# Attention and state-space background work of a hybrid decoder step: wider table products, softmax scaling and masks partly on ScalarE, sample values laid out by dimension, larger portions

## The chip, the cores and the metric

One core of one Trainium2 chip. The metric is the device time of one execution in microseconds, from the first to the last instruction with what lies around it, as the median of several runs.

## The reference

One layer of a decoder for 512 prompt tokens behind 16 meta tokens (528 rows) and 8 sample tokens (each one new position with its own cache), with shared weights, all in float32:

```python
xn = rmsnorm(x, norm_gain)                       # 536 rows of 2048
h = xn @ w_in                                    # 2048 x 8704
q, k, v, z_a, u, z_s, g_a, g_s = split(h)        # 16 query heads and 4 key heads of 64
q, k = rope(rmsnorm(q)), rope(rmsnorm(k))
# attention: window of 128, 16 meta tokens always visible, one sink per head
s = where(mask, q @ k.T / 8, -inf)
m = maximum(max(s), sink)
w = exp(s - m) / (sum(exp(s - m)) + exp(sink - m))
o = w @ v                                        # prompt in blocks of 128; a sample token: 16 + 127 + 1 keys
# S5 branch: 64 groups of 16 channels, 64 complex states each
h_t = lam_bar * h_(t-1) + b_bar @ u_t
y = gelu(real(c @ h_t) + d_skip * u)
y = y * sigmoid(y @ w_glu + b_glu)
br_a = (o * silu(z_a)) @ w_attn_out
br_s = (y * silu(z_s)) @ w_ssm_out
out = x + (sigmoid(g_a) * br_a + sigmoid(g_s) * br_s) @ w_out
```

Returned are `out` of prompt and sample, the last keys and values of the prompt, the shifted caches of the sample, and the final states.

## The kernel before

**The main line** is a long row of matrix products on TensorE. Activations lie with features on the partitions and the tokens as columns, in two halves of 268 (260 where the meta tokens are left out). Each float32 operand is split in a rounded high part and a rest (`xh`, `xl`; `whi` by ScalarE in L784, `wlo` by VectorE in L785), and a product is three matmuls: high by high, low by high, high by low. A weight tile of 128 x 1024 comes from `Stream` (L784, L785) with three buffers and two tiles ahead. Between them lies a **half unit**: one weight tile, 8 x 3 x 2 = 48 matmuls (L901). `ORDER1` lists which output blocks are made in which order: `x` blocks (gates, two half units each; evacuated to DRAM by `evac`), `u` blocks (input of the state space) and `h` blocks (keys, values, queries; `heads`, which holds a square `t` until its pair is there). What `ORDER1` leaves of the 48 x blocks follows; then come the GLU (8 half units), the state-space output (16), the attention output (16), and the last product L1264, in an arrangement with seven products for eight.

**Background.** Everything else hangs on that line by `Background`. Its lanes are generators: a step after each half unit grants a budget (`BUDGET` 4.0 while `ORDER1` runs, then `BUDGET2` 3.6, `BUDGET3` 2.2, `BUDGET4` 3.4), and portions are taken from lane 0, then lane 1, until the granted credit is used; each `yield` tells what the portion before it cost, and `yield None` ends a lane's turn. Lane 0 has the state-space preparation, eight `ssm` (one for each u block: `ssm_consts`, `ssm_block` and the gelu), `attention`, and at the end `attended`, which multiplies and splits the attention output. Lane 1 has `sample`. Instructions are put in each engine's queue by a scheduler that follows its own time line (`schedule_with_timeline_sim=True`); where two are ready, that of the earlier program text goes first. The weights' loads, casts and rests and the evacuations are given priority. Blocks `with self.later()` go behind the last matmul of the half unit just issued.

**State space.** For each u block, `ssm_consts` builds among other things the rotation table `tab` by outer products (`outer`, L297, on `rt1`, `rt2`), and `ssm_block` projects (L345, L346), rotates, scans, rotates back and projects out (L388 to L396).

**Attention.** `attention` starts when the pool of the state space is given back: it loads constants, the key rows (`keys`: `load`, `rope`, split into `KH`, `KL`), the values (`values`: copies `vb`, `mt`, five transposes on TensorE in L505 and L506, then `V`, `Vm`) and the queries of a head group (`load_q`, `queries`: `QT`). The row buffers `sb`, `sw`, `rb` are double. For each of 4 head groups and 4 blocks, `blocks` runs: `scores` (L537, L538: matmuls, copied to `S`, the previous block's part merged by mask), `softmax` (maximum, `Exp` with sums on ScalarE in L556, division into `Pn`, `Pm`), `turn` (transposes in L573, L574; `po` the own block's masked part, `pm` the meta part by head, `pp` the previous block's part) and `weigh` (L591: 4 matmuls for each of `po`, `pm`, `pp`). `weigh` of a block comes one portion after its `turn`, `turn` after the next block's `scores`.

**Sample.** `sample` has 128 rows (8 tokens by 16 heads). Keys come in 16 loads of 9 positions on the POOL queue (`load`, L677), are multiplied and summed (L685, L686); softmax; values come in 16 loads of 9 positions, are multiplied (L701), summed over a strided view (L703) and added up (L705).

Of the kernel before, what the change touches and what calls it, by code (L numbers as in the profile page):

```python
# [14 lines left out]
P = 128  # L15
# [208 lines left out]
def ssm_consts(nc, pool, psum, R, D, ub, a_bT, a_bN, a_cT, bdm):  # L224
# [70 lines left out]
    def outer(dst, i, j):  # L295
        for a in range(4):
            v.tensor_tensor(out=dst[:, a], in0=bc(x[:, i, a], 2, 12), in1=bc(y[:, j, a], 1, 11), op=ALU.mult)  # L297
# [4 lines left out]
    yield 2.3  # L302
# [11 lines left out]
    yield 2.3  # L314
# [106 lines left out]
class Attn:  # L421
    def __init__(self, nc, pool, psum, dram, C, oT, raw, rk, rq, later):
# [3 lines left out]
        self.V = [pool.tile([P, 256], F32, name=f"V{i}", bufs=1) for i in range(4)]  # L426
# [7 lines left out]
        self.QT = {}  # L434
# [91 lines left out]
    def scores(self, kv, b):  # L526
# [6 lines left out]
        for j in range(2):  # L533
# [8 lines left out]
            prev = ps[:, :, 0:128] if b else bc(C["neg"], 1, 2)  # L542
# [3 lines left out]
    def softmax(self, kv, S):  # L546
# [17 lines left out]
        v.tensor_tensor(out=Pn, in0=S[:, :, 16:144], in1=bc(den, 2, P), op=ALU.mult)  # L564
# [3 lines left out]
    def turn(self, kv, b, Pn, Pm):  # L568
# [9 lines left out]
        v.tensor_tensor(out=self.pm[0:64], in0=bc(ps[0:64, 1, 0:128], 1, 4), in1=bc(C["bd64"], 2, P), op=ALU.mult)  # L578
        parts = [(self.V[b], po), (self.Vm, self.pm)]
        if b:  # L580
            pp = pool.tile([P, 4, P], F32, name="pp", bufs=1)
            v.tensor_tensor(out=pp, in0=pt, in1=po, op=ALU.subtract)
            parts.append((self.V[b - 1], pp))
        return parts

    def weigh(self, kv, b, parts):
        nc = self.nc
        pv = self.psum.tile([P, 2, 512], F32, name="aux")
        for i, (V, pr) in enumerate(parts):
            for e in range(2):  # L590
                nc.tensor.matmul(pv[64 * e:64 * e + 64, 0, 0:256], lhsT=V[:, 64 * kv:64 * kv + 64], rhs=pr[:, e::2],  # L591
                                 start=(i == 0), stop=(i == len(parts) - 1))
# [4 lines left out]
    def blocks(self, kv, last):  # L597

        for b in range(4):
# [7 lines left out]
            if held:  # L607
                with self.later():
                    parts = self.turn(*held, *self.P)
                yield 1.8  # L610
                yield None
                with self.later():
                    self.weigh(*held, parts)
            self.P = self.softmax(kv, S)
            yield 2.0
        if last:
# [3 lines left out]
            yield 1.8  # L620
# [4 lines left out]
    def sample(self, a_sink, a_kc, a_vc):  # L625
# [48 lines left out]
        def load(i, c, src):  # L674
            t = pool.tile([P, CK, 64], F32, name="cache")
            n = CK if c < 15 else CK - 1
            self.after = nc.gpsimd.dma_start(out=t[:, 0:n], in_=src[:, c * CK:c * CK + n]).ins  # L677
            if n < CK:
                new = self.kD[i].rearrange("s b (e d) -> (s b e) d", e=2)
                for r in range(4):  # L680
                    nc.gpsimd.dma_start(out=t[r::4, n], in_=new)
            return t
        for c in range(16):
            t = load(0, c, a_kc)
            v.tensor_tensor(out=t, in0=t, in1=bc(self.qv, 1, CK), op=ALU.mult)  # L685
            v.tensor_reduce(out=s[:, c * CK:(c + 1) * CK], in_=t, axis=AX.X, op=ALU.add)  # L686
            yield 1.3
# [10 lines left out]
        op = pool.tile([P, 64], F32, name="o_p", bufs=1)  # L698
# [740 lines left out]
```

## Time and profile before

| | |
|---|---|
| three runs | 1316.38, 1316.45, 1317.16 us, median 1316.45 |
| profiled execution | 1317.95 us, its span 1316.1 us |
| PE, weight loads | busy 1300.7 and 1259.9 us |
| DVE | 1003.5 us in 1882 instructions |
| ACT, POOL | 443.5 and 52.4 us |
| granted clock of TensorE | 0.997 on average |
| DMA | 209.70 MB, 159 GB/s on average |

PE is TensorE, DVE VectorE, ACT ScalarE, POOL GpSimd, SP the engine whose queue issues most transfers. A row of a group of instructions reads: line, engine, operation, written tile <- read tiles, shape, count | busy time in all, mean of one in ns | idle time of the engine just before them and who ended it. A busy time counts overlapping instructions once, so a pipelined matmul has a mean of some 285 ns and starts every 120. The chain of waits follows the program back from its end; a piece of it is given as start, length, engine, line, count.

### The profile page before, as it was taken

Reading aid. Unit: us, or ns where it says so; the run is one execution under the profiler, and the core shown is the slowest. Engines: PE = TensorE matmul, PEld = TensorE weight load, DVE = VectorE, ACT = ScalarE, POOL = GpSimd, SP = SyncE. Lnnn points to the kernel's source line nnn. Section 1 sums busy time; section 2 is a strip of 40 time slices with the busy share of each in tenths; the row PEclk is TensorE's granted clock in tenths of the full one; section 3 lists DMA queues with packets and bytes.
Section 4 is the critical chain, followed back from the end, with each engine's and each line's share of the span. In section 5 each row is a group of like instructions: output and inputs, shape, how many; then the busy total and the mean of one; then the engine's idle time right before and its main releaser. Section 6 shows DMA issues by size and latency. Waiting matters only on the chain.

```text
span 1316.1 us, 26574 instructions
## 1 busy us (share of the span) xinstructions
PE 1300.7 (99%) x10804; PEld 1259.9 (96%) x10804; DVE 1003.5 (76%) x1882; ACT 443.5 (34%) x742; POOL 52.4 (4%) x124
## 2 busy tenths in 40 slices
PE   9999999999999999999989999999999999999998
PEld 8999999999999999999989999999999999999998
DVE  7887788887969697968577688686885357888775
ACT  8322221223222222222254433334433133344342
POOL 0000000000000000000400210100011000000000
PEclk9999999999999999999989999999999999999999
DMA  8347363626353444343874346446677666554441
GB/s 268 123 136 212 104 186 115 187 92 184 110 166 116 155 122 153 97 152 125 190 228 131 107 153 193 131 133 205 194 226 247 203 194 189 159 199 142 151 145 50
DMA packets 95962, 209.70 MB, mean 159 GB/s; under 512 B 16556, under 2 KB 34972, under 8 KB 95808
## 3 DMA queue, kind: packets, MB, share of 16 engines
q1 hardware_dynamic: 91168, 194.11, 46.8%
q0 software_dynamic: 4672, 13.89, 4.0%
q8 instruction: 85, 1.39, 0.4%
q14 instruction: 37, 0.30, 0.1%
HBM read 175.32 MB, written 34.74 MB: 160 GB/s over the span
## 4 chain that ended last, share of the span: by engine, by line
PE 91%; DMA 3%; DVE 2%; ACT 1%; SPq 1%; issue 0%; POOL 0%; DVEq 0%; POOLq 0%; ACTq 0%
PE mm L901 70%; PE pr L1264 12%; PE aux L591 2%; PE mm L988 1%; DMA sw<-rawD 1%; PE aux L537 1%; PE aux L345 1%; PE aux L346 1%; PE aux L538 1%; PE aux L1065 1%; PE mm L1186 1%; PE aux L392 1%; PE aux L573 1%; DMA gD<-z 1%; DMA sb<-rawD 0%; ACT xh L979 0%
## 5 line engine op out<-in xcount | busy, mean ns | idle before, releaser
L901 PE MATMUL mm<-xh,whi 128*128 128x260 f32 (+1 forms) x2048 | 421.4, 286 | 0.0
L901 PE MATMUL mm<-xh,wlo 128*128 128x260 f32 (+1 forms) x2048 | 417.6, 285 | 0.0
L901 PE MATMUL mm<-xl,whi 128*128 128x260 f32 (+1 forms) x2048 | 416.3, 284 | 0.0
L784 ACT CAST whi<-raw 128x1024 fp32r<-128x1024 f32 (+3 forms) x188 | 186.1, 995 | 520.8 <-PE mm L901 346.7
L901 PEld LDWEIGHTS mm<-xh,whi 128*128 128x128 f32 x2048 | 318.2, 189 | 9.7 <-issue 9.3
L901 PEld LDWEIGHTS mm<-xl,whi 128*128 128x128 f32 x2048 | 318.5, 189 | 3.9 <-issue 3.9
L901 PEld LDWEIGHTS mm<-xh,wlo 128*128 128x128 f32 x2048 | 316.1, 188 | 4.2 <-issue 4.1
L785 DVE TENSOR_TENSOR wlo<-raw,whi 128x1024 fp32r<-128x1024 f32 (+3 forms) x188 | 215.5, 1151 | 43.8 <-ACT whi L784 41.8
L1264 PE MATMUL pr<-cb,whi 128*128 128x260 f32 x896 | 161.8, 283 | 1.3 <-DVE t L1244 1.3
L1264 PEld LDWEIGHTS pr<-cb,whi 128*128 128x128 f32 x896 | 138.1, 188 | 2.1 <-ACT whi L840 1.7
L901 PE MATMUL mm<-Y,whi 128*128 128x260 f32 x768 | 125.5, 284 | 0.0
L1264 PE MATMUL pr<-cb,wlo 128*128 128x260 f32 x448 | 125.5, 283 | 0.0
L901 PEld LDWEIGHTS mm<-Y,whi 128*128 128x128 f32 x768 | 105.7, 188 | 2.3 <-issue 2.3
L841 DVE TENSOR_TENSOR wlo<-raw,whi 128x1024 fp32r<-128x1024 f32 x56 | 67.1, 1223 | 23.0 <-ACT whi L840 21.3
L1264 PEld LDWEIGHTS pr<-cb,wlo 128*128 128x128 f32 x448 | 84.0, 188 | 0.0
L901 PE MATMUL mm<-A,whi 128*128 128x260 f32 x512 | 82.2, 282 | 0.0
L901 PE MATMUL mm<-Y,wlo 128*128 128x260 f32 x384 | 77.6, 283 | 0.0
L840 ACT CAST whi<-raw 128x1024 fp32r<-128x1024 f32 x56 | 57.7, 1049 | 55.1 <-DVE raw L839 21.0
L901 PEld LDWEIGHTS mm<-A,whi 128*128 128x128 f32 x512 | 70.2, 188 | 0.0
L928 DVE TENSOR_TENSOR z<-mm,R 128x520 f32<-128x520 f32 x43 | 30.0, 697 | 44.1 <-PE mm L901 42.5
L901 PEld LDWEIGHTS mm<-Y,wlo 128*128 128x128 f32 x384 | 59.2, 188 | 0.4 <-issue 0.4
L901 PE MATMUL mm<-A,wlo 128*128 128x260 f32 x256 | 51.6, 283 | 0.0
(377 smaller groups left out, 1496.6 us busy)
## 6 DMA issues: line engine op xcount, KB each, us to landing
raw<-in_w SPq DMA_DIRECT2D x202, 512.0 KB, 3.8
gD<-z SPq DMA_DIRECT2D x48, 260.0 KB, 2.2
t<-gD SPq DMA_DIRECT2D x32, 260.0 KB, 2.8
cache<-in_kc POOLq DMA_DIRECT2D x15, 288.0 KB, 3.5
cache<-in_vc POOLq DMA_DIRECT2D x15, 288.0 KB, 3.3
xr<-in_x SPq DMA_DIRECT2D x16, 268.0 KB, 5.5
sD<-z SPq DMA_DIRECT2D x16, 260.0 KB, 2.1
z<-sD SPq DMA_DIRECT2D x16, 260.0 KB, 3.0
```

Of the source, the lines that this page charges most:

```text
L345: nc.tensor.matmul(bu[:, i, 0:272], lhsT=D["bh"][:, i, a], rhs=U[:, a], start=True, stop=False)
L346: nc.tensor.matmul(bu[:, i, 0:272], lhsT=D["bl"][:, i, a], rhs=U[:, a], start=False, stop=True)
L392: nc.tensor.matmul(y[32 * a:32 * a + 32, 0, 0:NE], lhsT=D["cl"][:, a, i], rhs=H[:, a, i, 0:NE], start=False, stop=(i == 1), skip_group_che ...
L537: nc.tensor.matmul(ps[:, e, 0:272], lhsT=q, rhs=KH[:, k0:k0 + 272], start=True, stop=False)
L591: nc.tensor.matmul(pv[64 * e:64 * e + 64, 0, 0:256], lhsT=V[:, 64 * kv:64 * kv + 64], rhs=pr[:, e::2], start=(i == 0), stop=(i == len(part ...
L784: nc.scalar.copy(out=hi, in_=raw)
L785: self.dve = nc.vector.tensor_tensor(out=lo, in0=raw, in1=hi.bitcast(F32), op=ALU.subtract).ins
L840: nc.scalar.copy(out=hi, in_=t)
L841: nc.vector.tensor_tensor(out=lo, in0=t, in1=hi.bitcast(F32), op=ALU.subtract)
L901: m = nc.tensor.matmul(ps[:, c, 0:W], lhsT=wt[:, k], rhs=xo(kt, c), start=f, stop=l)
L928: v.tensor_tensor(out=z, in0=ps, in1=R_[:, :, 8:CH], op=ALU.mult)
L1264: nc.tensor.matmul(bank, lhsT=wt[:, p], rhs=cb[p][:, e, x], start=first and f and p == 0, stop=l and p == 7, skip_group_check=not first an ...
```

## The change

Five parts.

- `outer` in `ssm_consts` makes one product of 528 elements instead of four of 132.
- `Pn` is made by four scaled copies on ScalarE instead of one product on VectorE; so is `pm`. `pp` is now a plain copy of the whole transposed block on ScalarE, no longer its difference from `po`; in exchange `po` is weighed with the differences of the V rows, `V[b] - V[b-1]`, made once per head group (`dV`, one buffer, on VectorE). `neg` has one column.
- Sample values lie by dimension: a load brings 4 dimensions of 143 positions, product and sum run over contiguous elements, and the new position's value (`vn`) is added at the end.
- Declared costs: table portions 2.3 to 2.1, `turn` 1.8 to 0.8, sample 1.3 to 1.5. Budgets: 4.0 to 4.6 and 3.6 to 4.0.
- `ORDER1`: a u block after every four blocks instead of every five. Eight more x blocks come after the list.

```diff
     def outer(dst, i, j):
-        for a in range(4):
-            v.tensor_tensor(out=dst[:, a], in0=bc(x[:, i, a], 2, 12), in1=bc(y[:, j, a], 1, 11), op=ALU.mult)
+        v.tensor_tensor(out=dst, in0=bc(x[:, i], 3, 12), in1=bc(y[:, j], 2, 11), op=ALU.mult)
...
-    yield 2.3
+    yield 2.1
...
-        self.V = [pool.tile([P, 256], F32, name=f"V{i}", bufs=1) for i in range(4)]
+        self.VV = pool.tile([P, 4, 256], F32, name="V", bufs=1)
+        self.V = [self.VV[:, i] for i in range(4)]
...
-            prev = ps[:, :, 0:128] if b else bc(C["neg"], 1, 2)
+            prev = ps[:, :, 0:128] if b else C["neg"].unsqueeze(2).to_broadcast([P, 2, P])
...
-        v.tensor_tensor(out=Pn, in0=S[:, :, 16:144], in1=bc(den, 2, P), op=ALU.mult)
+        for r in range(4):
+            nc.scalar.activation(out=Pn[:, r], in_=S[:, r, 16:144], func=AF.Copy, scale=den[:, r:r + 1])
...
-        v.tensor_tensor(out=self.pm[0:64], in0=bc(ps[0:64, 1, 0:128], 1, 4), in1=bc(C["bd64"], 2, P), op=ALU.mult)
-        parts = [(self.V[b], po), (self.Vm, self.pm)]
+        for r in range(4):
+            nc.scalar.activation(out=self.pm[0:64, r], in_=ps[0:64, 1, 0:128], func=AF.Copy, scale=C["bd64"][:, r:r + 1])
+        parts = [(self.D[kv][b], po), (self.Vm[:, 64 * kv:64 * kv + 64], self.pm)]
         if b:
             pp = pool.tile([P, 4, P], F32, name="pp", bufs=1)
-            v.tensor_tensor(out=pp, in0=pt, in1=po, op=ALU.subtract)
-            parts.append((self.V[b - 1], pp))
+            nc.scalar.copy(out=pp, in_=pt)
+            parts.append((self.V[b - 1][:, 64 * kv:64 * kv + 64], pp))
...
-                yield 1.8
+                yield 0.8
                 yield None
                 with self.later():
                     self.weigh(*held, parts)
+            if b == 0:
+                ks = slice(64 * kv, 64 * kv + 64)
+                dv = self.pool.tile([P, 3, 64], F32, name="dV", bufs=1)
+                self.nc.vector.tensor_tensor(out=dv, in0=self.VV[:, 1:4, ks], in1=self.VV[:, 0:3, ks], op=ALU.subtract)
+                self.D[kv] = [self.VV[:, 0, ks]] + [dv[:, i] for i in range(3)]
...
+        new = [kD[i].rearrange("s b (e d) -> (s b e) d", e=2) for i in range(2)]
+        vn = pool.tile([P, 64], F32, name="vn", bufs=1)
+        for r in range(4):
+            nc.gpsimd.dma_start(out=vn[r::4], in_=new[1])
...
         for c in range(16):
-            t = load(1, c, a_vc)
-            v.tensor_tensor(out=t, in0=t, in1=bc(s[:, c * CK:(c + 1) * CK], 2, 64), op=ALU.mult)
-            dst = op if c else o[:, 0]
-            v.tensor_reduce(out=dst, in_=t.rearrange("p k d -> p d k"), axis=AX.X, op=ALU.add)
-            if c:
-                v.tensor_tensor(out=o[:, 0], in0=o[:, 0], in1=op, op=ALU.add)
-            yield 1.3
+            t = pool.tile([P, 4, NK - 1], F32, name="cache")
+            self.after = nc.gpsimd.dma_start(out=t, in_=a_vc[:, 4 * c:4 * c + 4]).ins
+            v.tensor_tensor(out=t, in0=t, in1=bc(s[:, 0:NK - 1], 1, 4), op=ALU.mult)
+            v.tensor_reduce(out=o[:, 0, 4 * c:4 * c + 4], in_=t, axis=AX.X, op=ALU.add)
+            yield 1.5
+        v.scalar_tensor_tensor(out=o[:, 0], in0=vn, scalar=s[:, NK - 1:NK], in1=o[:, 0], op0=ALU.mult, op1=ALU.add)
...
-BUDGET = 4.0
-BUDGET2, BUDGET3, BUDGET4 = 3.6, 2.2, 3.4
+BUDGET = 4.6
+BUDGET2, BUDGET3, BUDGET4 = 4.0, 2.2, 3.4
...
-for _u in range(8):
-    ORDER1 += [("u", _u), ("x", 0), ("x", 0)]
-    ORDER1 += [("h", 2 * _u), ("h", 2 * _u + 1)] if _u < 6 else [("x", 0), ("x", 0)]
+for _u in range(0, 8, 2):
+    ORDER1 += [("u", _u), ("x", 0)] + [("h", 3 * _u // 2 + i) for i in range(2)]
+    ORDER1 += [("u", _u + 1), ("x", 0), ("x", 0), ("h", 3 * _u // 2 + 2)]
```

The host's layout of the value cache and the order of the weight tiles follow.

More of the change, by code (lines that the diff above doesn't have):

```diff
@@ L673, in sample @@
         s = pool.tile([P, NK], F32, name="ssc", bufs=1)
[L674 removed]
+        new = [kD[i].rearrange("s b (e d) -> (s b e) d", e=2) for i in range(2)]
+        vn = pool.tile([P, 64], F32, name="vn", bufs=1)
+        for r in range(4):
+            nc.gpsimd.dma_start(out=vn[r::4], in_=new[1])
+        for c in range(16):
             t = pool.tile([P, CK, 64], F32, name="cache")
             n = CK if c < 15 else CK - 1
[L677 removed]
+            nc.gpsimd.dma_start(out=t[:, 0:n], in_=a_kc[:, c * CK:c * CK + n])
             if n < CK:
[L679 removed]
                 for r in range(4):
[L681 to L684, printed above, removed]
+                    nc.gpsimd.dma_start(out=t[r::4, n], in_=new[0])
             v.tensor_tensor(out=t, in0=t, in1=bc(self.qv, 1, CK), op=ALU.mult)
             v.tensor_reduce(out=s[:, c * CK:(c + 1) * CK], in_=t, axis=AX.X, op=ALU.add)
[L687 removed]
+            yield 1.5
         m = pool.tile([P, 4], F32, name="m")
```

16 lines of the change are left out of this document (8 added, 8 removed).

## The prediction

> **What bounds the kernel now.** I read the page first, then TensorE's waits, then the busy times by stretches, then the chain of waits in the attention stage.
>
> ```profile
> span 1316.1 us, 26574 instructions
> PE 1300.7 (99%) x10804; PEld 1259.9 (96%) x10804; DVE 1003.5 (76%) x1882; ACT 443.5 (34%) x742; POOL 52.4 (4%) x124
> PE aux L505 <- DVE vb L501: 5.3, 1, 5.3
> PE aux L537 <- DVE QT L522: 1.3, 1, 1.3
> PE pr L1264 <- DVE t L1244: 1.3, 1, 1.3
> 991.85 149.95 PE mm L901 x1248
> 400.00:420.00 20.00, 20.00 (x159) 18.67 (x159) 19.86 (x31) 6.12 (x9) 0.35 (x3) 1.00 0.34 107
> 115.00:625.00 510.00, 510.00 (x4377) 492.29 (x4376) 416.20 (x825) 135.32 (x169) 3.26 (x28) 1.00 0.46 140
> 655.40:661.10 5.70, 0.43 (x5) 0.22 (x3) 5.37 (x12) 2.60 (x7) 0.00 (x0) 0.77 0.84 265
> 661.00:665.30 4.30, 4.26 (x20) 4.22 (x21) 4.16 (x10) 3.02 (x9) 0.00 (x0) 0.50 0.66 196
> 690.00:890.00 200.00, 200.00 (x1607) 185.81 (x1606) 151.10 (x286) 76.08 (x202) 21.01 (x40) 1.00 0.45 140
> 890.00:992.00 102.00, 102.00 (x830) 96.19 (x829) 79.35 (x136) 42.52 (x94) 8.07 (x15) 1.00 0.69 215
> 1140.00:1160.00 20.00, 18.66 (x149) 17.92 (x149) 18.96 (x23) 9.96 (x12) 0.00 (x0) 1.00 0.47 168
> ```
>
> (The stretches' columns: length, then busy time of PE, weight loads, DVE, ACT, POOL, then granted clock, DMA share, GB/s.) TensorE is the bound in every stage. Undisturbed it starts a matmul every 149.95 / 1248 = 0.120 us, and it is idle for only 1316.1 - 1300.7 = 15.4 us of the span. VectorE at 76% is not the bound: at 400 to 420 us it is busy 19.86 of 20 us and TensorE still loses nothing. So an instruction taken from VectorE gains nothing by itself. The change can move the time in two ways: by idle time of TensorE, and by how its matmuls are interleaved.
>
> The one large loss in the middle is the start of attention. TensorE stands 5.3 us before the transposes of `values` (L505). When it resumes, it runs 4.3 us at a granted clock of 0.50 and gets 20 matmuls done where 4.3 / 0.120 = 36 would fit: another 16 x 0.120 = 1.9 us. With the 1.3 us before L537 the place costs 5.3 + 1.9 + 1.3 = 8.5 us. The clock falls after 5.3 us of idleness; the 1.3 us before L1264 lie in the stretch from 1140 us, which keeps 1.00. The Trainium skill (TensorE: Matmul & The Clock Gate, Part 1: The HAM clock gate) says that one idle window of about 3.4 us halves the clock until a busy window has passed; the trace agrees, between 1.3 us without a fall and 5.3 us with one.
>
> **Work that only moves between engines or in time.** The rows of one instruction:
>
> ```profile
> L785 DVE TENSOR_TENSOR wlo<-raw,whi 128x1024 fp32r<-128x1024 f32 x80 | 97.4, 1218 | 17.1 <-ACT whi L784 17.1
> L297 DVE TENSOR_TENSOR rt<-T,T 128x132 f32<-128x132 f32 x128 | 29.2, 288 | 0.1
> L350 DVE TENSOR_TENSOR p<-aux,tab 128x528 f32<-128x528 f32 x32 | 22.5, 704 | 23.0 <-PE aux L346 22.2
> L564 DVE TENSOR_TENSOR Pn<-S,den 128x512 f32<-128x512 f32 x16 | 11.0, 690 | 0.4
> L577 DVE TENSOR_TENSOR po<-aux,k_mown 128x512 f32<-128x512 f32 x16 | 11.0, 686 | 9.2 <-PE aux L574 9.2
> L578 DVE TENSOR_TENSOR pm<-aux,k_bd 64x512 f32<-64x512 f32 x16 | 10.8, 672 | 0.0
> L582 DVE TENSOR_TENSOR pp<-aux,po 128x512 f32<-128x512 f32 x12 | 8.1, 676 | 0.0
> L703 DVE TENSOR_REDUCE o_p<-cache 128x64 f32<-128x576 f32 x15 | 17.8, 1186 | 0.1
> L686 DVE TENSOR_REDUCE ssc<-cache 128x9 f32<-128x576 f32 x16 | 11.9, 746 | 0.1
> L705 DVE TENSOR_TENSOR o_s<-o_s,o_p 128x64 f32<-128x64 f32 x15 | 3.3, 218 | 0.1
> L594 ACT COPY oT<-aux 128x128 f32<-128x128 f32 x32 | 6.9, 267 | 30.7 <-PE aux L591 30.7
> L930 ACT ACTIVATE z<-z 128x520 f32<-128x520 f32 x16 | 10.2, 637 | 3.3 <-DVE z L928 3.2
> ```
>
> Rotation tables: 128 products of 132 elements (29.2 us) become 32 of 528, at L350's 22.5 us: VectorE saves 6.7 us. Sample values: the reduction over a strided view (1186 ns) becomes one over contiguous elements, taken as L686's 746 ns: 16 x 0.44 = 7.0 us, and L705's 3.3 us go; one fused add comes. Attention: `Pn`, `pm` and `pp` leave VectorE, 11.0 + 10.8 + 8.1 = 29.9 us; four small differences of V rows (`dV`) come, under 0.7 us each by L564. ScalarE gets 64 + 64 scaled copies of 128 columns at L594's 0.267 us and 12 copies of 512 at L930's 0.637: 34.2 + 7.6 = 41.8 us. All these are worth nothing on TensorE's path as long as that has matmuls ready: its number of instructions is unchanged. `dV` has one buffer, so its write waits for the `weigh` of the head group before; behind it on VectorE stand the maximum of the next softmax and the next `wlo`, three times, and `wlo` is made two weight tiles (2 x 48 x 0.120 = 11.5 us) ahead. The POOL queue keeps its 40 loads for the sample; the four of `vn` wait for `kD` and stand ahead of later key loads, which serve only that off-path lane.
>
> Larger portions: a state-space block declares 38.6 before and gets 10 half units of 4.0; afterwards two declare 76.4 and get 16 of 4.6, with the rest running over. Counting the portions through, the first of attention comes after half unit 78 instead of 90, that of the first scores after 85 instead of 97, and attention's last after 122 instead of 141. In the state-space stage VectorE has 416.2 us of work in 510 us (82%). Afterwards 12 half units (12 x 48 x 0.120 = 69 us) are gone from the stage, and of the work 6.7 us of products, 12 x 1.22 = 14.6 of `wlo` and, for six x blocks with two operations of L564's 0.69 each, 8.3: 387 of 441 us, 88%. That is below the 99% at which the stretch from 400 us loses nothing. Heads of a pair now stand up to three blocks apart and hold one of the two `t` buffers; evacuating through the other takes 0.64 + 2 x 0.69 us of a block's 11.5, so nothing. In attention, ScalarE has 76.1 + 42.5 = 118.6 us of work in 302 us (39%); afterwards at most 160 us in 37 / 44 of that time, 254 us: 63%. Its `whi` casts have the 11.5 us of cover. I take 0 for all of this, with 3 us against as the other end: two waits such as those before L537 and L1264.
>
> **What does reach TensorE: `weigh` in fewer stretches.** In the chain of waits each uninterrupted run of `weigh` matmuls (L591) is one piece:
>
> ```profile
> 699.23 0.58 PE aux L591 x4
> ...
> 849.78 0.58 PE aux L591 x4
> 850.36 0.43 PE mm L901 x2
> 850.79 0.58 PE aux L591 x4
> 851.38 0.55 PE mm L901 x3
> 851.93 0.58 PE aux L591 x4
> ...
> 970.25 1.45 PE aux L591 x12
> ...
> 986.28 0.58 PE aux L591 x4
> ```
>
> A block's 12 records take 1.45 us in one go, and 3 x 0.58 = 1.74 in three. Between them two main matmuls take 0.43 instead of 0.24, and three 0.55 instead of 0.36. So being split in three costs 0.29 + 0.19 + 0.19 = 0.67 us, 0.33 per interruption. From the first row to the last I count 36 pieces for 16 blocks, so at most 20 interruptions can go: 6.6 us. They come from VectorE making `po`, `pm`, `pp` one after the other: ready 0.69, 1.36 and 2.03 us after the transposes, while one group occupies TensorE 0.58 us. Afterwards `po` stays on VectorE (0.69) and `pm` runs beside it on ScalarE (4 x 0.267 = 1.07): ready before `po`'s group ends at 1.27, so the first interruption can close. `pp` follows `pm` on ScalarE (1.07 + 0.64 = 1.71) and would be ready before the second group ends at 1.85. Against this, a `whi` cast or an exponential can stand in ScalarE's queue between them, and scheduled order, not readiness alone, decides. Between 0 and 20 I take 9, about half: 9 x 0.33 = 3.0 us. The other end is a loss of the same kind: ten more pieces if ScalarE makes `pm` late, 3.3 us.
>
> The Trainium skill (ScalarE: Activation LUTs, Rules for kernel authors) speaks against the move: multiplications and additions belong on VectorE, and ScalarE is for functions. For the single operation the rows agree: 4 x 0.267 = 1.07 us on ScalarE against 0.69 for `Pn`. By the rule the sum would have a loss in place of the 3.0 us, as rival 4 prices it.
>
> **The start of attention.** The stall is a queue of transfers:
>
> ```profile
> sw<-rawD SPq DMA_DIRECT2D x8, 67.0 KB, 6.9
> 657.10 3.37 DMA sb<-rawD
> 660.49 0.49 DVE L501 COPY vb<-sb 128x256 f32<-128x256 f32 x2 [0.27 <-DMA sb<-rawD]
> 667.25 0.49 DVE L501 COPY vb<-sb 128x256 f32<-128x256 f32 x2
> ```
>
> The key rows take 6.9 us to land among the constants, the first sample caches and the weights; `values` needs the buffers that the keys free. All of that starts when the state-space pool is released, in both kernels, with the same loads and the same two buffers. `keys`, `values` and `load_q` keep their portions and their text. So I leave the 8.5 us where they are, only some 70 us earlier. Their place in TensorE's order comes from the scheduler that fixes the queues when the program is built, by its own durations, so the stall can come out otherwise: the bounds are all of it gone and rival 3's growth.
>
> **The sum.** The profiled execution took 1317.95 us, 1.85 around its span, and 1.5 (0.11%) above the median of 1316.45. 1317.95 - 3.0 = 1314.95 for a profiled execution, and 1313.5 us against the median, 0.23% faster. Differences below 0.2% (2.6 us) I count as no change: about what a measurement of this kernel can tell.
>
> **Rivals.**
> 1. *Forecast* (0.42): stall kept, 5 to 14 interruptions closed: 1311.8 to 1314.8 us.
> 2. *The stall goes* (0.16). The transposes land later in TensorE's order, or the rows earlier. Short of the idle time that halves the clock, about 5.3 + 1.9 = 7 us go; the wait before L537 is next. With the 3 us of merging 1306 us, without it 1309. For it: the stall rests on a mismatch of a few us between order and transfers. Against: nothing in the chain of transfers is changed.
> 3. *The stall grows* (0.24), the case on the slower side. Both `values` portions now fall after the same half unit (81), before after 93 and 94. If TensorE's order puts the second five transposes right behind the first, it waits from the end of the first copies (660.98) to that of the second (667.74), less five transposes at half clock (5 x 4.3 / 20 = 1.1 us): 5.7 us, then 1.9 more at half clock, and the wait before L537 again: 1313.5 + 5.7 + 1.9 + 1.3 = 1322.4 us. It decides once the second wait is longer than the 3 us that merging gives. Against: the first transposes already stood where their data was expected, not where they were issued.
> 4. *ScalarE becomes late* (0.06): 41.8 / 16 = 2.6 us more ScalarE work per block; if a tenth shows on TensorE, 4.2 us in all, without merging: 1320.7 us. Against: at most 63% load and 11.5 us of cover. This is how the rule of the Trainium skill (ScalarE: Activation LUTs, Rules for kernel authors) would come out.
> 5. *Nothing reaches TensorE* (0.12): the pieces stay near 36 and the stall as it is: 1316.5 us, within 2 us.
>
> **How the numbers follow.** Of the forecast's 0.42 I put 0.12 above 1313.8 us, within 0.2%. Faster: 0.30 + 0.16 = 0.46. Same: 0.12 + 0.12 = 0.24. Slower: 0.24 + 0.06 = 0.30. The range runs from rival 2 with merging to rival 3, 1306 to 1322 us. The forecast's own range is 1311 to 1316.
>
> **What would show it.** In the changed profile: TensorE still at 99% with its 10804 instructions; the L591 pieces of the chain counted, 27 by the forecast, above 34 wrong; the wait before the transposes of `values` again 4 to 7 us, with one stretch at clock 0.50; VectorE's busy time down by 35 to 50 us and ScalarE's up by about 42; no wait of TensorE on `whi`, `pm` or `pp` above 1 us; the last `weigh` before the last of the 48 x blocks. A new wait of more than 3 us anywhere after the warm-up, or a second stretch at half clock, makes the prediction wrong on the slow side.

## The result, and the profile after

The changed kernel takes **1326.32 us** (median of 4 runs, 1325.37 to 1327.07) beside 1316.41 us for the kernel before on the same chip: a ratio of 1.0075, 95% interval 1.0057 to 1.0092. It is 9.9 us slower. The forecast was 1313.5 us with a range of 1306 to 1322, so the time lies outside the range, on the slower side.

The profiled execution took 1326.37 us. Its span and busy times, from the page of the changed kernel:

```profile
span 1324.6 us, 26577 instructions
PE 1304.9 (99%) x10804; PEld 1259.5 (95%) x10804; DVE 967.9 (73%) x1732; ACT 484.1 (37%) x882; POOL 52.3 (4%) x124
```

The engines' work moved as forecast: VectorE has 35.6 us less (forecast 35 to 50 less), ScalarE 40.6 us more (forecast 42). TensorE's 10804 instructions are unchanged. What it waited for, in the changed kernel (line waited for <- what ended the wait: us in all, times, longest):

```profile
PE aux L391 <- DVE H L377: 6.6, 1, 6.6
PE aux L505 <- DVE vb L501: 2.8, 1, 2.8
...
PE pr L1270 <- DVE t L1250: 1.3, 1, 1.3
...
PE aux L537 <- DVE QT L522: 0.7, 1, 0.7
```

The wait at L505 was 5.3 us before and is 2.8 us. On top stands a wait of 6.6 us that the kernel before did not have. The stretches behind these waits (columns as in the prediction):

```profile
533.90:540.80 6.90, 0.28 (x7) 0.09 (x6) 6.90 (x9) 0.73 (x1) 0.00 (x0) 0.70 0.36 126
540.80:544.00 3.20, 3.20 (x32) 1.42 (x32) 2.40 (x8) 0.64 (x1) 0.00 (x0) 0.57 0.11 21
584.50:588.00 3.50, 3.50 (x19) 3.50 (x18) 3.43 (x7) 1.54 (x7) 0.00 (x0) 0.51 0.64 190
```

TensorE is nearly idle in the first stretch while VectorE is busy all of it, and there are two stretches near half clock after the warm-up, at 540.8 and at 584.5 us.

To see where a kernel gains or loses, I add up, from TensorE's records, the time from each matmul of background work to the start of the next matmul; where a main matmul goes over to background work, its usual 0.12 us counts as main. Waits and half clock so fall to the work at which they stand. Differences to the kernel before in us, each from one profiled execution:

| | changed kernel | amount before |
|---|---|---|
| state-space output (`y`: L387, L391, L395) | +8.0 | 19.6 |
| values and scores (the start of attention) | -4.0 | 25.3 |
| `weigh` (L593) | +5.4 | 27.7 |
| state-space constants and the sums in `heads` | -1.4 | 11.7 |
| main matmuls, without the last product | +0.3 | 1035.7 |
| all else | +0.2 | 196.1 |
| span | +8.4 | 1316.1 |

So there are two large losses, `y` and `weigh`, and one large gain, smaller than either. The profiled execution of the kernel before was itself 1.5 us above its median, so the differences add up to 8.4 us and not to the 9.9 us of the medians; this holds for all such sums below.

**The place of the 6.6 us.** VectorE's timeline in the changed kernel (start, length, engine, line, operation). L1059 is the evacuation of the last h block, L1084 begins `head_norms` for keys and then for queries, L369 is a scan of the state space, L934 the evacuation of an x block:

```profile
507.59 0.70 DVE L1059 TENSOR_TENSOR z<-mm,R 128x520 f32<-128x520 f32 x1 [3.71 <-PE mm L907]
...
514.62 0.18 DVE L1084 TENSOR_SCALAR z<-z 67x32 f32<-67x32 f32 x1 [0.88 <-DMA z<-skD]
...
523.66 0.19 DVE L1084 TENSOR_SCALAR z<-z 128x65 f32<-128x65 f32 x1
...
525.86 2.35 DVE L369 TENSOR_TENSOR_SCAN w<-d,w 128x1056 f32<-128x1056 f32 x1
...
533.94 2.35 DVE L369 TENSOR_TENSOR_SCAN w<-d,w 128x1056 f32<-128x1056 f32 x1
...
541.45 0.69 DVE L934 TENSOR_TENSOR z<-mm,R 128x520 f32<-128x520 f32 x1
...
544.64 0.70 DVE L934 TENSOR_TENSOR z<-mm,R 128x520 f32<-128x520 f32 x1 [1.10 <-DMA rqD<-z]
```

`head_norms` takes its two tiles `r1` and `r2` as `ev.tile(..., name="z")`. `z` has two buffers, and `evac` of an x block writes into `z` as well. From 514.6 to 541.4 us both belong to the norms. In the new `ORDER1` two x blocks follow the last h block directly; their matmuls ended at 521.6 and 533.6 us, their evacuations come at 541.45 and 544.64, and until then both PSUM banks of the main line (the two places that its matmuls can write to) are taken. TensorE's queue goes on with matmuls of `y`, of which L391 waits for `H`; that name stands in the row, but the next x block would not have had a bank before 541.45 + 0.69 = 542.1 us either.

Before, the same norms took as long, and TensorE lost nothing by it (VectorE in the kernel before):

```profile
478.75 0.67 DVE L1053 TENSOR_TENSOR z<-mm,R 128x520 f32<-128x520 f32 x1
...
486.64 0.17 DVE L1078 TENSOR_SCALAR z<-z 67x32 f32<-67x32 f32 x1
...
493.11 0.72 DVE L1098 TENSOR_TENSOR uf<-mm,R 128x536 f32<-128x536 f32 x1
...
514.33 0.70 DVE L928 TENSOR_TENSOR z<-mm,R 128x520 f32<-128x520 f32 x1
```

There a u block followed the last h block. It leaves its bank through `uf`, at 493.11, and TensorE always had one bank.

**`weigh` in more pieces.** The chain of waits in the changed kernel (start, length, what), and ScalarE's timeline just before:

```profile
692.86 0.58 PE aux L593 x4
693.44 1.15 PE mm L907 x8
694.60 0.57 PE aux L593 x2
695.17 0.32 PE mm L907
695.49 0.58 PE aux L593 x2
```

```profile
688.70 0.42 ACT L556 ACTIVATE S<-S,nm 128x144 f32<-128x144 f32 x1 [2.72 <-DVE nm L553]
...
689.91 0.40 ACT L556 ACTIVATE S<-S,nm 128x144 f32<-128x144 f32 x1
...
690.39 1.12 ACT L580 ACTIVATE pm<-aux,k_bd 64x128 f32<-64x128 f32 x4
```

In this block `pm` stands in ScalarE's queue behind the four exponentials of the next softmax, and then comes out head by head; half of its four matmuls needs heads 0 and 2, the other half heads 1 and 3. TensorE's order has `pm` in two halves here and in four other blocks of the 16. In TensorE's records I count 47 uninterrupted runs of `weigh` (36 of four matmuls, 10 of two, 1 of twelve), before 36 (31 with four, 2 of eight, 3 of twelve). A run of two costs 0.66 to 0.78 us, 0.72 on average, as much as one of four with 0.67.

### The profile page after: what moved, and what is told of

It reads as the page before. It is cut to its first block, busy times and chain, and to the rows that moved or that the text cites. A ratio compares the mean times of both kernels' runs of the same rounds, so it can differ in the third digit from the quotient of the medians.

```text
span 1324.6 us, 26577 instructions
## 1 busy us (share of the span) xinstructions
PE 1304.9 (99%) x10804; PEld 1259.5 (95%) x10804; DVE 967.9 (73%) x1732; ACT 484.1 (37%) x882; POOL 52.3 (4%) x124
## 4 chain that ended last, share of the span: by engine, by line
PE 87%; DMA 5%; DVE 4%; issue 1%; ACT 1%; SPq 1%; DVEq 0%; ACTq 0%
PE mm L907 67%; PE pr L1270 12%; PE aux L593 2%; PE mm L994 1%; DMA xr<-in_x 1%; PE aux L537 1%; PE aux L344 1%; PE aux L345 1%; PE aux L538 1%; PE aux L391 1%; DMA gD<-z 1%; DMA k_qg<-in_qg 1%; PE aux L574 1%; DVE wlo L791 1%; PE aux L1071 0%
## 5 line engine op out<-in xcount | busy, mean ns | idle before, releaser
L934 DVE TENSOR_TENSOR z<-mm,R 128x520 f32<-128x520 f32 x43 | 29.9, 696 | 66.2 <-PE mm L907 65.1
L1223 DVE SCALAR_TENSOR_TENSOR z<-t,mm 128x520 f32<-128x520 f32 x16 | 11.1, 696 | 57.1 <-PE mm L907 57.1
```

The source lines that it names most:

```text
L934: v.tensor_tensor(out=z, in0=ps, in1=R_[:, :, 8:CH], op=ALU.mult)
```

## Experiments

All were timed beside the kernel before, in four groups; its medians there were 1316.70, 1316.29, 1316.28 and 1316.42 us. The table has the median, the ratio to the kernel before with its 95% interval, and the sums as above (start: values and scores; differences to the kernel before, one profiled execution each).

| kernel | us | ratio (interval) | `y` | start | `weigh` | main |
|---|---|---|---|---|---|---|
| a_norm_own | 1322.89 | 1.0050 (1.0032 to 1.0069) | +0.6 | +2.0 | +4.6 | +0.1 |
| b_x_behind | 1317.72 | 1.0007 (0.9997 to 1.0016) | +0.3 | -0.4 | -0.2 | -0.2 |
| a_pm_vector | 1322.89 | 1.0045 (1.0028 to 1.0062) | +8.2 | -2.8 | +1.2 | -0.4 |
| b_scalar_parts | 1320.99 | 1.0030 (1.0017 to 1.0043) | 0.0 | -0.4 | +3.0 | +0.2 |
| b_xx_behind | 1322.97 | 1.0052 (1.0037 to 1.0067) | +0.3 | -2.7 | 0.0 | +1.8 |
| b_order | 1320.06 | 1.0032 (1.0018 to 1.0046) | +0.6 | +0.9 | +1.5 | +0.5 |
| a_norm_pm | 1319.46 | 1.0025 (1.0014 to 1.0036) | +0.6 | +1.0 | +1.2 | 0.0 |
| b_both | 1309.07 | 0.9943 (0.9927 to 0.9960) | 0.0 | -6.7 | -4.8 | +2.6 |
| b_offpath | 1318.48 | 1.0013 (1.0003 to 1.0022) | +0.3 | +0.1 | -2.2 | +4.5 |
| b_start | 1309.27 | 0.9952 (0.9936 to 0.9969) | 0.0 | -8.1 | 0.0 | -1.7 |
| b_weigh | 1313.56 | 0.9984 (0.9975 to 0.9993) | 0.0 | +1.7 | -4.1 | +1.7 |
| a_all | 1306.19 | 0.9931 (0.9916 to 0.9947) | +0.6 | -6.8 | -4.8 | +0.7 |
| b_order_outer | 1323.34 | 1.0051 (1.0036 to 1.0066) | +8.2 | -2.4 | +1.5 | +0.3 |
| a_outer_narrow | 1320.63 | 1.0033 (1.0019 to 1.0047) | +0.6 | -2.0 | +3.9 | +0.3 |
| a_all2 | 1312.76 | 0.9970 (0.9959 to 0.9981) | +0.6 | -4.1 | -4.8 | +4.0 |

In b_xx_behind the wait falls to the state-space constants (+5.3), which have no column. The profiled executions of b_offpath (1320.73) and b_weigh (1317.23) were the longest of their runs, so their sums lie above their medians.

### The wait of 6.6 us

**a_norm_own**: the changed kernel with buffers of their own for the norms.

```diff
-            r1 = ev.tile([p, n], F32, name="z")
-            r2 = ev.tile([p, n], F32, name="z")
+            r1 = sp.tile([p, n], F32, name="hn1", bufs=1)
+            r2 = sp.tile([p, n], F32, name="hn2", bufs=1)
...
-            rsqrt_dve(nc, ev, r2, r1, [p, n], "t", "")
+            rsqrt_dve(nc, sp, r2, r1, [p, n], "hn", "t")
```

> The changed kernel, with the work tiles of head_norms (r1, r2, t) in buffers of their own instead of the two z and t buffers that the evacuation of the x blocks uses. Theory (the two z buffers: the block behind the last h block can't leave PSUM until both norms are through, so TensorE has no bank for the next block): the 6.6 us wait in the state-space projection at 534 us goes, with the half clock behind it, 8 us in all: 1326.3 to 1318 us, and the evacuation of the x block behind the last h block comes within 3 us of its matmuls. Rival (VectorE, 88% loaded by the larger portions, has the states H late): the wait stays at 4 us or more and the time above 1323 us.

The x block that had to wait until 541.45 is evacuated 20 us earlier (VectorE's timeline), and the 6.6 us are gone from TensorE's waits:

```profile
521.64 0.70 DVE L934 TENSOR_TENSOR z<-mm,R 128x520 f32<-128x520 f32 x1 [0.62 <-PE mm L907]
```

```profile
PE aux L505 <- DVE vb L501: 4.1, 2, 3.8
PE aux L537 <- DVE QT L522: 3.9, 2, 2.0
```

`y` falls from +8.0 to +0.6, which is what the buffers were held to cost. But the time falls only by 3.4 us instead of 8, because the start of attention now waits 8.0 us again, with half clock: -4.0 becomes +2.0.

**b_x_behind** and **b_xx_behind**: the kernel before, with only the order of three blocks after the last h block changed, first one and then both x blocks ahead of the last u block but one.

```diff
-    ORDER1 += [("u", _u), ("x", 0), ("x", 0)]
+    ORDER1 += [("x", 0), ("u", _u), ("x", 0)] if _u == 6 else [("u", _u), ("x", 0), ("x", 0)]   # b_x_behind
+    ORDER1 += [("x", 0), ("x", 0), ("u", _u)] if _u == 6 else [("u", _u), ("x", 0), ("x", 0)]   # b_xx_behind
```

> The kernel before with one edit in ORDER1: the last h block is followed by an x block and then by the u block, instead of the other way round. Budgets, portions and engines as before. Theory (the two z buffers): a wait of 3 to 8 us and a stretch at half clock appear soon after the last h block, 1316.4 to 1321 to 1326 us. Rival (only the load of VectorE makes the wait): no wait, 1316.4 us within 2.

> The kernel before, with one line of ORDER1 changed: the last u block stands behind two x blocks instead of ahead of them, so that the last h block is followed by two blocks whose evacuation needs a `z` buffer; nothing of the larger portions, of ScalarE's part or of the outer products. Theory (the two `z` buffers, held by the norms of the heads, keep both banks of the projections): the third block waits for a bank until the norms are through, a wait of 5 to 8 us that the `bu` and `y` matmuls only partly fill, with a stretch at half clock behind it; 1321 to 1325. Rival (the larger portions of the state space on VectorE are needed for the wait, the order alone does nothing): 1316.5, no wait over 1.5 us between 480 and 520 us.

With one x block behind, nothing measurable happens, where a wait was expected: it is evacuated at 510.21, but the u block gave its bank back at 504.75. With two, the wait is there in a kernel with no other edit (waits of TensorE, the stretch behind, and VectorE's evacuations of the last h block and of the first x block):

```profile
PE mm L901 <- DVE t L417: 5.3, 1, 5.3
```

```profile
510.00:516.00 6.00, 6.00 (x29) 6.00 (x30) 2.32 (x4) 1.13 (x2) 0.00 (x0) 0.54 0.27 97
```

```profile
478.56 0.67 DVE L1053 TENSOR_TENSOR z<-mm,R 128x520 f32<-128x520 f32 x1
...
509.12 0.70 DVE L928 TENSOR_TENSOR z<-mm,R 128x520 f32<-128x520 f32 x1
```

Here the row names a step of the norms itself (L417), and a main matmul as the one that waits.

**b_order**, **b_order_outer**, **a_outer_narrow**: is the order enough? b_order has `ORDER1` and the two budgets of the change and nothing else; b_order_outer has the wider products of `outer` (and their cost of 2.1) besides; a_outer_narrow is the changed kernel with the four narrow products and the cost of 2.3.

```diff
-for _u in range(8):
-    ORDER1 += [("u", _u), ("x", 0), ("x", 0)]
-    ORDER1 += [("h", 2 * _u), ("h", 2 * _u + 1)] if _u < 6 else [("x", 0), ("x", 0)]
+for _u in range(0, 8, 2):
+    ORDER1 += [("u", _u), ("x", 0)] + [("h", 3 * _u // 2 + i) for i in range(2)]
+    ORDER1 += [("u", _u + 1), ("x", 0), ("x", 0), ("h", 3 * _u // 2 + 2)]
```

```diff
-        for a in range(4):
-            v.tensor_tensor(out=dst[:, a], in0=bc(x[:, i, a], 2, 12), in1=bc(y[:, j, a], 1, 11), op=ALU.mult)
+        v.tensor_tensor(out=dst, in0=bc(x[:, i], 3, 12), in1=bc(y[:, j], 2, 11), op=ALU.mult)
```

> The kernel before with the changed kernel's ORDER1 and its two budgets (4.6 and 4.0) alone: no wider products, no work moved to ScalarE, caches as before. Theory: the order and the portions carry the whole `y` loss of the changed kernel (+8.0 us) and also its shorter start of attention (-2.9 in the values, -1.7 in the selection of keys), while the pieces of `weigh` stay at about 36: 1320 to 1321. Rival (it takes the moved engine work as well): 1316.5, no wait of 5 us before the second half of the inputs' projection.

> The kernel before with the changed kernel's order of blocks and budgets, and with its wider products for the rotation tables and their smaller cost in the planner; nothing of the attention. Theory (the order gives the chance, the cheaper products move the scans in between the norms' steps): the norms take some 27 us instead of 13.5, TensorE waits 5 to 7 us at about 534 us with a stretch at half clock behind it, y +8; the start of attention waits less, as in the changed kernel; 1320 to 1324. Rival (something else of the change brings them there): no wait at 534 us, and the time of the order alone, 1320, with a wait of 7 us at the start of attention.

> The changed kernel with the products for the rotation tables as they were, four instructions each, and their old cost in the planner. Theory: the scans fall behind the norms' steps again, no wait at 534 us (y +0.6 instead of +8.0), but the wait at the start of attention comes back at 7 us: 1322 to 1324. Rival (the order and budgets do it together with the attention's changes): the wait at 534 us stays, 1326.

b_order missed: it loses, but not where I said (`weigh` +1.5, the start +0.9, with a wait of 7.0 us there). Its two x blocks stand behind the last h block too, yet the norms are through in 13.5 us (VectorE, first step of the norms and evacuation of the x block):

```profile
515.62 0.18 DVE L1078 TENSOR_SCALAR z<-z 67x32 f32<-67x32 f32 x1 [3.28 <-DMA z<-skD]
...
529.11 0.70 DVE L928 TENSOR_TENSOR z<-mm,R 128x520 f32<-128x520 f32 x1
```

No scan lies in between, where the changed kernel has two of 2.35 us with their rotations. With the wider products the scans are there and the evacuation comes at 541.12 (VectorE in b_order_outer; below it TensorE's waits):

```profile
541.12 0.69 DVE L927 TENSOR_TENSOR z<-mm,R 128x520 f32<-128x520 f32 x1
```

```profile
PE aux L391 <- DVE H L377: 6.6, 1, 6.6
PE aux L504 <- DVE vb L500: 5.1, 1, 5.1
```

And with the narrow products the changed kernel is rid of the wait, its x block evacuated at 529.53, and 5.7 us faster by the medians; this is better than expected, as the start of attention waits 4.9 us and not 7. So the wait needs three things: both x blocks behind the last h block, norms and evacuation in the same two buffers, and norms that last longer than the two x blocks occupy TensorE (23 us). From the evacuation of the last h block to that of the first x block it is 20.7 us in b_order and 21.4 us in a_outer_narrow, which don't wait, and 33.9 us in b_order_outer and the changed kernel, which do. What stretches the norms need not be scans: b_xx_behind has 30.6 us and the wait, and no scan between the norms' steps, but products for the state-space constants and `wlo`. Whether the lower cost in the planner or the shorter duration of the products brings the scans in was not separated.

### The pieces of `weigh`

**a_pm_vector** is the changed kernel with `pm` made by VectorE in one instruction; **b_scalar_parts** is the kernel before with `Pn`, `pm`, `pp` on ScalarE, `dV` and the one column of `neg`, as in the change; costs, budgets and order as before.

```diff
-        for r in range(4):
-            nc.scalar.activation(out=self.pm[0:64, r], in_=ps[0:64, 1, 0:128], func=AF.Copy, scale=C["bd64"][:, r:r + 1])
+        v.tensor_tensor(out=self.pm[0:64], in0=bc(ps[0:64, 1, 0:128], 1, 4), in1=bc(C["bd64"], 2, P), op=ALU.mult)
```

> The changed kernel with pm back on VectorE as one product; Pn and pp stay on ScalarE. Theory (pm stands behind the four exponentials of the next softmax in ScalarE's queue and comes out head by head, so weigh is cut into 47 pieces instead of 36): the pieces fall to 36 or fewer, the pieces of two records vanish, and the time falls by 11 x 0.33 = 3.6 us to 1322.7. Rival (the cutting comes from the earlier, denser portions): 44 pieces or more, 1326 us within 1.5.

> The kernel before with the ScalarE part of the change alone: Pn, pm and pp on ScalarE, po with the differences of V, neg with one column; order, budgets and declared costs as before. Theory (ScalarE's queue cuts weigh into more pieces): 44 to 50 pieces and 3 to 4 us more: 1320 us. Rival (nothing on the path): 36 pieces, 1316.4 us within 1.5. By the forecast on record it would be 27 pieces and 1313.4 us.

With `pm` on VectorE no run of two is left: 41 runs instead of 47 (36 or fewer were expected), `weigh` +1.2 instead of +5.4, and 3.4 us by the medians. The +1.2 left is much what order and budgets alone cost in b_order: +1.5, with 42 runs, none of two. The move to ScalarE by itself makes 41 runs out of 36 (44 to 50 were expected), six of them of two, and costs 3.0 us of `weigh` and 0.30% of the time. Fewer pieces, as forecast, came in neither.

**a_norm_pm** puts both repairs on the changed kernel.

> The changed kernel with both earlier repairs: the norms of the heads in buffers of their own, and pm made by VectorE in one instruction. If the two losses are independent, 1326.3 - 3.4 - 3.4 = 1319.5, with the start of attention waiting again (about 8 us in two waits and two stretches at half clock) and some 41 pieces of weighing. If they overlap (the order of the blocks decides the pieces), 1321.5 to 1323.

1319.46 us, as the sum said: the two losses are independent. Against the kernel before 3.2 us are left by the medians; this profile, only 1.2 us longer than that before, has them in the start (+1.0), `weigh` (+1.2) and `y` (+0.6), with -1.4 in constants and sums against them.

**b_weigh**: the kernel before, with the weighing of a block issued at the start of the next block, when `po`, `pm` and `pp` are all made.

```diff
         for b in range(4):
             yield None
+            if self.ready:
+                with self.later():
+                    self.weigh(*self.ready)
+                self.ready = None
...
                 yield None
-                with self.later():
-                    self.weigh(*held, parts)
+                self.ready = *held, parts
```

> The kernel before with the second edit of that pair: the weighing of a block one portion later, when its three parts are ready. Theory: 16 pieces in place of 36, each 0.24 to 0.33 us: weighing -4.8 to -6.6, and no wait of 3.9 us later on, since the start is not moved: 1310 to 1312. Rival (the later weighing itself makes the late wait): 1314 to 1316.

Runs of twelve replace runs of four: 19 runs instead of 36 (16 in b_both), most of them together with the next block's scores. `weigh` falls by 4.1 us for 17 runs, in b_both by 4.8 for 20: 0.24 us per interruption, where I had taken 0.33. The time falls by 2.7 us only, between what was expected and its rival; its profile has new waits of 2.3 us in all before main matmuls, on the maximum of a softmax (L551), and of 1.0 us on its sums (L560).

### The start of attention

**b_start** is the kernel before with the five transposes of each `values` portion taken out and issued three portions behind the queries of the first head group (`vb` in a buffer of `S`, two of `mt`).

```diff
             yield from at.queries(kv)
+            if kv == 0:
+                for _ in range(3):
+                    yield None
+                for e in range(2):
+                    at.values_turn(e)
+                yield None
```

**b_both** adds b_weigh's edit. Both expectations:

> The kernel before with the first edit of the pair run together earlier: the transposes of the sample values behind those of the queries. Theory: the wait at the start of attention and its half clock go, values -5.9 as in the pair: 1310.5. Rival (half of the gain of the pair came with the other edit, the wait of 3.9 us at the change of projections with this one): 1314.

> The kernel before with two edits that the account of the losses points to. First, the transposes of the sample values at the start of attention are issued behind those of the queries and three more yields, so TensorE no longer stands before them (8.5 us of waits and half clock before). Second, the weighing of a block is issued one portion later, when all three of its parts are ready, so that a block is one piece of 12 records instead of two or three pieces (36 pieces become 16, at 0.33 us each: 6.6 us). If both hold: 1316.5 - 8.5 - 6.6 = 1301.4. If the wait at the start only moves to the queries or to the selection: 1310. If the pieces are no cost in themselves: 1308. If neither: 1316.5.

b_start does all that was hoped of it: the longest wait left after the warm-up is the old one near the end (TensorE's waits), and the granted clock is 1.000.

```profile
PE pr L1275 <- DVE t L1255: 1.3, 1, 1.3
```

b_both gains nothing more. `weigh` gives its 4.8 us, and a wait of 3.9 us with half clock behind it comes up at 896 us, in the GLU, where attention's work still runs beside it. ScalarE there:

```profile
892.07 1.26 ACT L526 CAST QT<-sb 64x512 fp32r<-64x512 f32 x2 [3.51 <-DVE sb L464]
893.93 1.05 ACT L794 CAST whi<-raw 128x1024 fp32r<-128x1024 f32 x1 [0.59 <-PE mm L911]
894.88 0.66 ACT L1219 ACTIVATE mm<-mm,k_bglu 128x520 f32<-128x520 f32 x1
```

The GLU's tanh (L1219) stands behind a query cast that waits 3.5 us for VectorE and a weight cast that waits for TensorE. This is read from the timelines; no run separates it.

### The rest of the change, and a faster version

**b_offpath**: the kernel before with the wider products and the sample values by dimension, and their costs; the second diff above, and of the sample:

```diff
-            t = load(1, c, a_vc)
-            v.tensor_tensor(out=t, in0=t, in1=bc(s[:, c * CK:(c + 1) * CK], 2, 64), op=ALU.mult)
...
+            t = pool.tile([P, 4, NK - 1], F32, name="cache")
+            self.after = nc.gpsimd.dma_start(out=t, in_=a_vc[:, 4 * c:4 * c + 4]).ins
+            v.tensor_tensor(out=t, in0=t, in1=bc(s[:, 0:NK - 1], 1, 4), op=ALU.mult)
```

> The kernel before with the changed kernel's wider products for the rotation tables and its layout of the sample values alone (their two costs in the planner with them): order of the blocks, budgets and ScalarE's part as before. Theory: off the path, 1316.5 within 1 us, with the wait for the values at the start of attention and 36 pieces of weighing as before. Rival (VectorE's lower load in the attention stage lets the parts come sooner): up to 1 to 2 us faster. Rival (the larger, longer value instructions stand ahead of the parts on VectorE): up to 2 us slower, in the weighing.

Not nothing: +2.2 us by the medians, and not in the weighing, which falls by 2.2 us. It has 27 runs instead of 36, the very number that the prediction forecast, with nothing moved to ScalarE. In its (long) profiled execution the loss is in the same GLU: a wait of 2.8 us, and then

```profile
912.50:916.00 3.50, 3.50 (x17) 3.50 (x18) 3.47 (x6) 1.72 (x4) 0.00 (x0) 0.51 0.40 138
```

half clock, 17 matmuls where 29 fit. The changed kernel, whose attention ends earlier, has no such wait. That this wait is the loss of the median execution too is not shown.

**a_all** is the changed kernel with the four repairs: buffers for the norms, `pm` on VectorE, b_start and b_weigh (with `dV` made after the weighing it must not overtake). **a_all2** has the transposes two portions behind the queries and no portion after:

```diff
-                for _ in range(3):
+                for _ in range(2):
                     yield None
                 for e in range(2):
                     at.values_turn(e)
-                yield None
```

> The changed kernel with all four repairs: the norms of the heads in buffers of their own, pm by VectorE, the transposes of the sample values behind the queries, the weighing one portion later. From 1319.5 (the first two), less 8 us of waits and half clock at the start, less 6 us of weighing: 1305.5. If the wait of 3.9 us at the change of projections comes as in the pair on the kernel before, 1310.

> The changed kernel with all four repairs, and the transposes of the sample values only two portions behind the queries instead of three, with no portion after them. If the wait of 3.5 us at the change of projections comes from attention ending two portions later, it shrinks or goes: 1302 to 1304. If the values are not laid out in time two portions earlier, a wait at the start returns: 1306 to 1310. If the places of the work at the change of projections are a matter of chance: 1304 to 1308.

a_all takes 1306.19 us, 10.1 us less than the kernel before beside it and 20 us less than the changed kernel in its own runs: the fastest kernel of this study. One wait of 3.5 us in the GLU is left, with half clock behind it. In a_all2 it is down to 1.6 us, at a price: a main matmul now waits 2.7 us for `wlo` at 583 us and the scores wait 2.0 us for `QT`, and at 1312.76 us, above all three expectations, it is 6.6 us slower than a_all by the medians.

## Why the prediction was wrong

**Work that only moves, taken at 0 with 3 us against: this is the step that failed first.** Its load forecast was right: 88% for VectorE in the state-space stage, and the changed profile has 382.78 of 436 us there, 88%. What didn't follow is "below the 99% at which the stretch from 400 us loses nothing". TensorE lost 6.8 us in a stage with that load. It did not wait for VectorE's capacity but for a buffer, as a_norm_own shows at the same order of blocks (`y` +0.6): the norms' 24 small steps hold `z` for as long as the larger instructions between them take. I had looked at which buffers the h blocks hold, but only at `t`, and only at the pair; `r1` and `r2`, with the name `z`, stand in the code I had read. The rows of before showed the price as well: the x block there was evacuated 35.6 us after the last h block (478.75 to 514.33), against 23 us that two x blocks take on TensorE.

**`weigh`, -3.0 us forecast, +5.4 measured: the sign was wrong.** The doubt was written down ("a `whi` cast or an exponential can stand in ScalarE's queue between them") and then half the gain was taken all the same. What was wrong is that ScalarE would have `pm` ready before `po`'s group ends; in five blocks its group is cut in two instead. The four exponentials stand shortly ahead of `pm` in four of these five, but also in four blocks that are not cut, so that they are the cause is likely and not shown; that `pm` on ScalarE is the cause, a_pm_vector shows. The bound against (ten more pieces, 3.3 us) was near in the number of pieces, 11, but not in their price: an interruption costs 0.24 us, a group of four cut in two halves 2 x 0.72 - 0.67 = 0.77. Six of the 11 come with order and budgets (42 runs in b_order), five are cut groups: 6 x 0.24 + 5 x 0.77 = 5.3 us. The Trainium skill (ScalarE: Activation LUTs, Rules for kernel authors) says that multiplications belong on VectorE; the runs agree with its verdict, at +0.30% for the move alone. In b_scalar_parts the whole loss lies in `weigh`, that is in the order in which the parts come, and not in the time of the copies.

**The start of attention, 8.5 us kept.** It neither stayed, nor went, nor grew. In the changed kernel it shrank by 4.0 us, and three kernels in which the other wait was taken away or never came (a_norm_own, a_norm_pm, b_order) have it back at +0.9 to +2.0; a_outer_narrow, without that wait too, has it at -2.0. The same loads and the same code gave waits at the transposes between 2.8 and 7.0 us. What sets it within this range was not settled. That the place is worth what the forecast said of it when it is cleared, b_start shows: 8.1 us in these sums, 7.0 by the medians.

**The rivals.** None was this one. Rival 3 (the start grows) didn't come. Rival 4 (ScalarE late) holds for a part: b_scalar_parts at 1320.99 is near the 1320.7 that it named, but by luck, since it took a tenth of ScalarE's added work where the profile shows +3.0 us of cut groups. Its 0.06 was too little, and it was not added to anything. The prediction's own test held: a new wait above 3 us and a second stretch at half clock were said to make it wrong on the slow side.

**What the sum should have been**: 8.0 for `y`, 5.4 for `weigh`, -4.0 at the start, -1.4 at constants and sums, 0.5 for the rest: +8.5 on a span that grew by 8.4.

## What to carry to other kernels

When blocks of work change their order, list for each pair of neighbours which rotating buffers they share by name and how long each holds one: a mean load of 88% says nothing on a buffer that a chain of small dependent steps holds through a busy queue. Compare the time that the chain holds it with the time that the blocks behind it keep TensorE busy. When work moves to a less busy engine, look at what stands ahead of it in that engine's queue at that moment, not at the share of time that it is busy. And a repair should be expected to show the next wait behind it: here two of the four repairs (own buffers, later weighing) gave back a good part of their gain somewhere else.

## What the runs showed of the hardware

Shorter idle times than expected halve the clock. In b_weigh TensorE waits 2.1 us for `QT` within the first stretch below, and then runs near half clock; the stretch of 1.7 us with little work at 940.5 us is followed by full clock:

```profile
673.40:675.70 2.30, 0.18 (x3) 0.01 (x1) 1.48 (x3) 0.36 (x1) 0.00 (x0) 1.00 0.87 291
675.70:680.20 4.50, 4.50 (x25) 4.50 (x26) 3.67 (x5) 1.50 (x3) 0.00 (x0) 0.64 0.68 168
940.50:942.20 1.70, 0.26 (x3) 0.07 (x2) 1.67 (x5) 0.13 (x1) 0.00 (x0) 1.00 0.62 158
942.20:946.20 4.00, 4.00 (x33) 4.00 (x34) 1.89 (x4) 3.73 (x12) 0.00 (x0) 1.00 0.54 181
```

In the middle of these 17 profiles every wait of TensorE of 2.7 us and more brought a stretch at half clock, none of 1.9 us and less did, and of the five between 2.0 and 2.2 us three did. The Trainium skill (TensorE: Matmul & The Clock Gate, Part 1: The HAM clock gate) gives one idle window of about 3.4 us; 2.1 us were enough here. In the kernel before, too, the clock did not wait for the end of the 5.3 us: the stretch from 655.40 us with its mean clock of 0.77 had (1 - 0.77) / 0.5 x 5.7 = 2.6 us at half clock, so it fell about 2.7 us after the last matmul's end at 655.8 us. A wait in this range has to be priced with more time behind it: 1.2 us where 19 matmuls were done and 29 fit (the changed kernel at 584.5 us), 1.9 us where it was 20 and 36 (the kernel before).
